# Two blocks of the up projection begun by token halves instead of three, one more by quarters; the context row by transfers, other planner prices, one more block of memory

## The chip, the cores and the metric

The kernel runs on one core of a Trainium2 chip. Its time is the device time of one execution in microseconds; the median of several executions is compared. The core has five engines, each with its own stream of instructions: TensorE (PE) multiplies matrices into eight banks of accumulator memory, VectorE (DVE) and ScalarE (ACT) work element by element, GpSimd (POOL) does the same more slowly, and SyncE (SP) mostly issues transfers between the large memory and the on-chip memory.

## The reference

One layer of a hybrid backbone over 512 latent tokens of width 1024, with 256 context tokens as a prefix. Cut to what matters:

```python
mod_x = split((silu(c)     @ w_mod + b_mod), 6)      # shift, scale, gate for latent tokens
mod_c = split((silu(c_ctx) @ w_mod + b_mod), 6)      # the same for context tokens
h_x = modulate(rms_norm(x,   mix_pre_norm), mod_x[0], mod_x[1]) @ w_in
h_c = modulate(rms_norm(ctx, mix_pre_norm), mod_c[0], mod_c[1]) @ w_in
mix = concat([latent_attention(...), ssd(...)]) @ w_out      # attention and a two-way state-space scan
x = x + mod_x[2] * rms_norm(mix, mix_post_norm)

h = modulate(rms_norm(x, ffn_pre_norm), mod_x[3], mod_x[4])
gate, val = split(h @ w_up, 2)                               # w_up: 1024 x (2 x 2816)
gate = depthwise_conv(gate, conv_w, conv_b)                  # width 3, along the tokens
ffn = (gelu(gate) * val) @ w_down                            # w_down: 2816 x 1024
x = x + mod_x[5] * rms_norm(ffn, ffn_post_norm)
```

All is float32. The kernel keeps that precision on TensorE by splitting each operand into a high and a low part (an ACT copy and a VectorE subtraction, `split`, lines 596 and 597) and adding three products: high x high, high x low, low x high.

## The kernel before

**An order worked out by a planner.** The program is traced twice. In the first pass every piece of memory is its own tile and the instructions are only listed. `plan` then finds the dependences between them, gives each instruction a cost (`price`) and places the pieces in `UNITS` units of 1 KB per partition (four make one block of 4 KB). A piece may reuse units only if the units' old users are modelled to end at least `MARGIN` ns before; units from `EDGE` on are kept for small pieces. A list scheduler, `Graph.schedule`, simulates the five engines and one DMA queue and writes the order of every engine; `plan` does this for 24 rounds, keeps the round with the shortest modelled time, and `refined` tries 1200 random shifts of priority on it. The second pass emits the instructions with each engine's order fixed. So an edit of one place can move instructions everywhere, and a constant of the model changes nothing but the order and the places in memory.

**The order of the stages.** The modulation of the first two chunks is computed while its weights arrive (to about 40 us), then the input projection, the scan and the attention pairs beside each other (to about 500), the output projection (L1436, 502 to 587), the up projection (588 to 830) and the down projection (L1764, to 930). The first 15 us hold matmuls on zeros (L786) that bring up TensorE's clock.

**The rows of `silu(c)`.** `cv` holds `c` in eight rows of 128 and `c_ctx` in eight more; lines 758 and 759 turn it into silu times two. `spread(i, v)` (line 766) copies one of the two over all 128 partitions: eight matmuls with a selecting column as the weight (L770) into a pair of banks, and one ACT copy of 1024 elements (L772). `spread(0, cs)` serves the latent tokens at the start, `spread(1, csc)` the context sums (`moddot`, L695) later.

**The up projection.** The hidden width 2816 is cut into 22 blocks of 128; each block has a gate half and a value half, so two 1024 x 128 weights. `up(j, ...)` with `gemm_T` (L861) computes a block plainly. The first `EARLY` = 3 blocks are begun on token rows 0 and 1 (256 tokens), while rows 2 and 3 are still being normalised (L1518, L1522) and transposed (`transposes`, L1530); their late halves follow. The transposes of rows 2 and 3 stand in the code ahead of the last early block. Each pair of banks comes from a list: what is freed goes to its end and what is needed is taken from its front.

The next 19 blocks follow the string `SEVEN`: 16 times "A", three times "P". "P" is the plain block of 512 tokens. "A" is `up_by_seven`: the product of the 2 x 2 quarters of weight and activation is made with seven quarter products instead of eight (Winograd's form of Strassen's scheme), each of 4 x 3 matmuls of 256 columns (`product`, L1646). It needs mixed activations, made once by `turn_h2` (sums L1597 to L1600, then wide splits), and mixed weights per block, made by `seven`: four loads, one of them an accumulating transfer issued from GpSimd (L1615) that adds two quarters on the way, then two sums on VectorE (L1625, L1626) and four splits. Partial products leave the banks by ACT (L1651) and VectorE (L1662, L1664, L1666). `gated` then does the convolution (L1566, L1567, L1569), gelu (L1571) and the product with the value half (L1573, L1574, or L1576 in a plain block), and for each pair of blocks the mixed operands of the down projection, which goes by seven products too (`sweep`, L1764).

**Small tiles.** `smalls` is a strip of 512 columns from which scalars are cut; `ones` is a 128 x 128 square of ones, read as a weight at L1047 and L1048 and as one column elsewhere.

Of the kernel before, what the change touches and what calls it, by code (L numbers as in the profile page):

```python
# [12 lines left out]
F32 = mybir.dt.float32  # L13
# [6 lines left out]
P = 128  # L20
D = 1024
# [52 lines left out]
    return c  # L74


UNITS, EDGE, MARGIN = 212, 168, 2500
STEP = {1: 1, 2: 2, 3: 4, 4: 4}

ON_PE = 2, 4, 6  # L80
# [1 line left out]
IDLE = 22, 26, 22  # L82
WIDE = 64
PACE = 1.9
TRIES = 1200
HOLD = 6
SEVEN = "AAAAAAAAAAAAAAAAPPP"


class Memory:  # L90
# [66 lines left out]
def price(x):  # L157

    ops = [(v.bass_ap.tensor.name, list(v.ap), v) for l in (x.outs, x.ins) for v in l if hasattr(v, "bass_ap")]
    size = lambda o: math.prod(c for _, c in o[1][1:])  # L160
    e, n = engine_of(x), max(map(size, ops))
    chip = all(not o[0].startswith("banks") for o in ops)
    kind = type(x).__name__
    if "DMA" in kind:
        n = size(ops[0]) * ops[0][1][0][1]
        runs = n // min(o[1][-1][1] for o in ops)
        return max(n * 4 / 360, runs * RUN / 16) * (2 if getattr(x, "cce_op", None) == ALU.add else 1)
    if e == "PE":
        if ops[1][2].dtype == mybir.dt.float32r:
            return (size(ops[1]) / (2.4 if size(ops[1]) >= 256 else 1.2) + 13) / (2 if ops[0][1][0][1] == 64 else 1)  # L170
        return max(107, size(ops[1]) / 1.2) if x.is_transpose else max(213, size(ops[1]) / 0.6)
    if "Memset" in kind:
        return 35 + 0.83 * n
    if e == "Activation":
        return 72 + (43 if chip else 0) + 93 * (len(ops) - 2) + 0.833 * n
    if e == "Pool":
        return 150 + (1.66 if any(not s for o in ops for s, c in o[1][1:] if c > 1) else 2.1) * n
    if "Predicated" in kind:
        return 69 + 1.02 * n
    if "Reciprocal" in kind:  # L180
        return 69 + 6.25 * n
    if "TensorScalar" in kind and chip and sum(size(o) > 1 for o in ops[1:]) < 2:
        return 69 + 0.52 * n
    return (130 if len(ops) == 4 or "TensorScalar" in kind and n > 1 and len(ops) == 3 else 69) + 1.04 * n
# [127 lines left out]
class Graph:  # L312
# [39 lines left out]
    def schedule(self, rank, look=0.06, back=False):  # L352

        eng, dma, cost, tables, shared = self.eng, self.dma, self.cost, self.tables, self.shared
        n, opens, after = len(cost), () if back else self.opens, self.before if back else self.after
        left = [len(b) for b in (self.after if back else self.before)]
        ready, start, end = [0.0] * n, [0.0] * n, [0.0] * n
        PE, SP, POOL, never = ENGINES.index("PE"), ENGINES.index("SP"), ENGINES.index("Pool"), float("inf")
        clock, order = [0.0 if back else BEGIN] * len(ENGINES), [[] for _ in ENGINES]
        later, now, due = [[] for _ in ENGINES], [[] for _ in ENGINES], [never] * len(ENGINES)  # L360
        ticks, held, port, queue, flying = {}, [0 if e == "Activation" else (4, 4) for e in ENGINES], 0.0, 0.0, []
        push, pop = heapq.heappush, heapq.heappop

        def turn(e):
            l, w, t = later[e], now[e], clock[e]
            while l and l[0][0] <= t:
                _, r, i = pop(l)
                push(w, (r, i))
            due[e] = t if w else l[0][0] if l else never

        for i in range(n):
            if not left[i]:
                ready[i] = max(0.0, rank[i] - AHEAD) if i in opens else 0.0
                push(later[eng[i]], (ready[i], rank[i], i))
        for e in range(len(ENGINES)):
            turn(e)
        for _ in range(n):
            while True:
                t = min(due)
                e = due.index(t)  # L380
                l, w = later[e], now[e]
                while l and l[0][0] <= t:
                    _, r, i = pop(l)
                    push(w, (r, i))
                r, i = pop(w)
                near, far, sooner = t + look * cost[i], t + 0.8 * cost[i], None
                for v in l:
                    if v[1] < r and v[0] < (near if v[1] > r - 5000 else far) and (sooner is None or v[1] < sooner[1]):
                        sooner = v
                if sooner is None:  # L390
                    break
                push(w, (r, i))
                clock[e] = sooner[0]
                turn(e)
            order[e].append(i)
            c, d = cost[i], dma[i]
            if not back and tables[i] not in (None, held[e]):
                held[e], t = tables[i], t + (TURN if e == PE else TABLE)
            if shared[i]:
                t = max(t, port)  # L400
                port = t + c
            if d and not back and len(flying) >= FLYING:
                t = max(t, flying[-FLYING])
            start[i] = t
            if d:
                began = t + d + DMA_START + (0 if e == SP else 2500 if e == POOL else 600)
                queue = max(began, queue) + c
                f = queue + DMA_ALONE * c
                if e != SP:
                    clock[e] = t + (1000 if e == POOL else 60)  # L410
                else:
                    if not back and t < DMA_FILLS:
                        f = max(began + (1 + DMA_ALONE) * c, queue - DMA_FULL)
                    clock[e] = t + d if back else max(t + d, queue - DMA_AHEAD)
                flying.append(f + DMA_WAIT)
            elif e == PE:
                f = t + c if back else self.product(t, i, ticks)
                clock[e] = f + 3
            else:
                clock[e] = f = t + c  # L420
            end[i] = f
            turn(e)
            for j, w in after[i]:
                if f + w > ready[j]:
                    ready[j] = f + w
                left[j] -= 1
                if not left[j]:
                    if j in opens:
                        ready[j] = max(ready[j], rank[j] - AHEAD)
                    push(later[eng[j]], (ready[j], rank[j], j))  # L430
                    turn(eng[j])
        return max(end), {e: o for e, o in zip(ENGINES, order)}, start, end
# [40 lines left out]
        return now  # L473


def plan(ins, pieces, hints, units, rounds=24):

# [16 lines left out]
                    preds[i].update(last)  # L496
    opens, shared = {u[0] for u in users.values()}, [ports(x) for x in ins]
    _, _, start, end, _ = Graph(preds, eng, dma, cost, share, tables, urgent, opens, shared).best()
    found = None
    for _ in range(rounds):  # L500
        held, types = [(-1, -1e9, [])] * units, [None] * (units // 4)
        inst, before = [((), -1e9)] * (units // 4), [((), -1e9)] * (units // 4)
        full, places = [set(p) for p in preds], []
        for t, (n, type_), at in pieces:
# [8 lines left out]
                        able.append(o)  # L513
                        free[o], due[o] = max(max(v[1] for v in h), (before if types[b] == type_ else inst)[b][1]), h

            fit = [o for o in able if free[o] + MARGIN <= s0]
            fit = [o for o in fit if (o >= EDGE) == (n < 3)] or fit
            if fit:
                o = max(fit, key=lambda o: sum(v[1] for v in due[o]) / len(due[o]))
# [17 lines left out]
        graph = Graph(full, eng, dma, cost, share, tables, urgent, opens, shared)  # L537
        now = graph.best()
        start, end = ([(p + q) / 2 for p, q in zip(*v)] for v in zip((start, end), now[2:4]))
        if found is None or now[0] < found[0][0]:  # L540
            found = now, places, graph
    now, places, graph = found
    now = graph.refined(now, TRIES)
    return now[0], places, now[1]


# [18 lines left out]
def build(nc, tc, ctx, a, out, dbg=None, places=None):  # L565
# [10 lines left out]
    def c_(shape, name, dt=F32):  # L576
        return cp.tile(list(shape), dt, name=name, tag=name, bufs=1)
# [9 lines left out]
    def load(dst, src, q=None):  # L587
        (q or nc.sync).dma_start(out=dst, in_=src)
# [16 lines left out]
        split(*w, raw, lo_eng)  # L605
        return w

    smalls = c_([P, 512], "smalls")

    def small(tag, w=1):  # L610
        cnt[0] += w
# [65 lines left out]

    sel = c_([P, 32], "sel", F32R)
    V.tensor_copy(sel, C("sel"))
    ones = c_([P, P], "ones")  # L680
    G.memset(ones, 1.0)


# [74 lines left out]
    act(th, cv, AF.Tanh, scale=0.5)  # L758
    V.scalar_tensor_tensor(out=cv, in0=th, scalar=1.0, in1=cv, op0=ALU.add, op1=ALU.mult)
    split(cvp[:16], cvp[32:48], cv)  # L760
    act(cch, cc, AF.Tanh, scale=0.5)
    V.scalar_tensor_tensor(out=cc, in0=cch, scalar=1.0, in1=cc, op0=ALU.add, op1=ALU.mult)
    V.tensor_scalar(out=cc, in0=cc, scalar1=0.5, scalar2=None, op0=ALU.mult)
# [63 lines left out]
    for i in range(NX):  # L827
        silu_of_z(0, zp, i)
    pfree(*za, pmod)
    spread(1, csc)  # L830
    zb = [pget("b"), pget("b"), pget("s"), pget("m")]
    mark = here()
    wz = [weight(a["wz"][k][:, 512:], 512) for k in range(KD)]
# [210 lines left out]
    pc, pt_ = pget("s"), pget("s")  # L1044
    mm(pc[:, :192], lhsT=C("trif"), rhs=fl(aF), start=True, stop=False)
    mm(pc[:, :192], lhsT=C("trib"), rhs=fl(aB), start=False, stop=True)
    mm(pt_[:, :192], lhsT=ones, rhs=fl(aF), start=True, stop=False)  # L1047
    mm(pt_[:, :192], lhsT=ones, rhs=fl(aB), start=False, stop=True)  # L1048
    V.tensor_copy(fl(cum), pc[:, :192])
    V.tensor_tensor(out=nb, in0=lnd, in1=cum, op=ALU.subtract)  # L1050
    V.tensor_tensor(out=fl(sw), in0=pt_[:, :192], in1=fl(nb), op=ALU.add)
# [500 lines left out]

    gT, mixed = [], []
    early, late = slice(0, 256), slice(256, 512)
    EARLY = 3

    h2v = lambda k, p_: h2[p_][k // 2][:, k % 2, :]

# [386 lines left out]
```

## Time and profile before

| what | us |
|---|---|
| median of three runs | 939.51 |
| lowest and highest of them | 938.52, 942.12 |
| the profiled execution | 939.16 |
| its span, first to last instruction | 937.4 |
| up projection, first matmul of L861 | 588.64 |
| output projection's last transposes and first early block: TensorE busy, 550 to 600 | 48.22 of 50 |
| down projection: TensorE busy, 850 to 900 | 49.21 of 50 |

The span is what the trace shows; the execution's own time is 1.76 us longer. The view by stages gives for each stretch the busy time of each engine; a "busy" TensorE means that at least one matmul was in flight, so spacing inside a run of equal matmuls, not the duration of one, is the price of a further one. A group's idle time is what the engine spent waiting just ahead of those instructions, with the releaser that ended it.

### The profile page before, as it was taken

Reading aid. Unit: us, or ns where it says so; the run is one execution under the profiler, and the core shown is the slowest. Engines: PE = TensorE matmul, PEld = TensorE weight load, DVE = VectorE, ACT = ScalarE, POOL = GpSimd, SP = SyncE. Lnnn points to the kernel's source line nnn. Section 1 sums busy time; section 2 is a strip of 40 time slices with the busy share of each in tenths; the row PEclk is TensorE's granted clock in tenths of the full one; section 3 lists DMA queues with packets and bytes.
Section 4 is the critical chain, followed back from the end, with each engine's and each line's share of the span. In section 5 each row is a group of like instructions: output and inputs, shape, how many; then the busy total and the mean of one; then the engine's idle time right before and its main releaser. Section 6 shows DMA issues by size and latency. Waiting matters only on the chain. (4 is left out here: it accounts for less than half of the span.)

```text
span 937.4 us, 16164 instructions
## 1 busy us (share of the span) xinstructions
PE 918.0 (98%) x5678; PEld 815.4 (87%) x5678; DVE 828.6 (88%) x1546; ACT 575.1 (61%) x1138; POOL 224.0 (24%) x230
## 2 busy tenths in 40 slices
PE   9999999999999999999999999999999999999997
PEld 8888898888888888879888888899999999888785
DVE  6999968888989888999999986997889889889998
ACT  4455336645688867868898224964455546357684
POOL 0001000565445665465520010100100000210011
PEclk9999999999999999999999999999999999999999
DMA  9943201114144333244669585924975755885883
GB/s 347 360 161 111 87 23 46 51 51 106 50 96 105 74 96 88 57 127 108 169 209 346 195 279 194 264 70 107 280 202 164 195 124 193 220 205 163 264 294 133
DMA packets 61552, 150.33 MB, mean 160 GB/s; under 512 B 8688, under 2 KB 11904, under 8 KB 61472
## 3 DMA queue, kind: packets, MB, share of 16 engines
q1 hardware_dynamic: 56784, 136.36, 45.7%
q0 software_dynamic: 3888, 11.27, 6.8%
q10 hardware_dynamic: 800, 1.68, 0.6%
q8 instruction: 44, 0.72, 0.3%
q14 instruction: 36, 0.29, 0.1%
HBM read 127.02 MB, written 6.34 MB: 142 GB/s over the span
## 5 line engine op out<-in xcount | busy, mean ns | idle before, releaser
L596 ACT ACTIVATE block<-block 128x512 fp32r<-128x512 f32 (+5 forms) x381 | 245.4, 681 | 144.9 <-DVE block L597 25.1
L597 DVE TENSOR_TENSOR block<-block,block 128x512 fp32r<-128x512 f32 (+4 forms) x357 | 276.7, 807 | 13.8 <-ACT block L596 9.1
L861 PE MATMUL banks<-block,block 128*128 128x512 f32 (+1 forms) x1364 | 277.8, 345 | 3.0 <-DVE smalls L635 1.8
L861 PEld LDWEIGHTS banks<-block,block 128*128 128x128 f32 x1364 | 214.4, 189 | 32.2 <-ACT block L596 3.7
L1646 PE MATMUL banks<-block,block 128*128 128x256 f32 x1344 | 168.3, 284 | 2.2 <-ACT block L596 1.0
L1646 PEld LDWEIGHTS banks<-block,block 128*128 128x128 f32 x1344 | 164.7, 192 | 4.1 <-ACT block L596 1.2
L1764 PE MATMUL banks<-block,block 128*128 128x512 f32 x462 | 109.5, 390 | 0.8 <-ACT block L596 0.6
L1764 PEld LDWEIGHTS banks<-block,block 128*128 128x128 f32 x462 | 86.4, 188 | 19.9 <-ACT block L596 1.2
L1308 PE MATMUL banks<-block,block 128*128 128x512 f32 (+1 forms) x384 | 102.4, 357 | 0.9 <-ACT block L1312 0.7
L596 ACT ACTIVATE block<-banks 128x512 fp32r<-128x512 f32 (+1 forms) x157 | 74.3, 494 | 30.6 <-PE banks L1324 18.9
L597 DVE TENSOR_TENSOR block<-banks,block 128x512 fp32r<-128x512 f32 (+1 forms) x157 | 85.0, 553 | 7.8 <-ACT block L596 7.1
L1436 PE MATMUL banks<-block,block 128*128 128x512 f32 x384 | 89.8, 391 | 0.0
L1436 PEld LDWEIGHTS banks<-block,block 128*128 128x128 f32 x384 | 71.5, 188 | 14.6 <-DVE block L1369 0.2
L1336 PE MATMUL banks<-block,block 128*128 128x256 f32 x384 | 70.1, 292 | 0.7 <-DVE block L1369 0.4
L1324 PE MATMUL banks<-cst,block 128*128 128x128 f32 x384 | 67.4, 274 | 1.1 <-DVE block L597 1.0
L1308 PEld LDWEIGHTS banks<-block,block 128*128 128x128 f32 x384 | 61.8, 189 | 6.8 <-ACT block L1312 1.5
L1310 DVE TENSOR_REDUCE smalls<-banks 128x1 f32<-128x768 f32 x64 | 60.8, 950 | 7.7 <-PE banks L1308 6.9
L695 DVE SCALAR_TENSOR_TENSOR block<-block,block 128x1024 f32<-128x1024 f32 x52 | 63.5, 1234 | 1.8 <-DMA block<-in_wmod_dram 1.8
L1312 ACT ACTIVATE block<-banks,smalls 128x768 f32<-128x768 f32 x64 | 57.8, 903 | 10.4 <-DVE smalls L1310 9.6
L890 DVE SCALAR_TENSOR_TENSOR block<-banks,cwh,block 128x511 f32<-128x511 f32 (+3 forms) x88 | 52.8, 623 | 11.7 <-ACT block L886 10.7
L1336 PEld LDWEIGHTS banks<-block,block 128*128 128x128 f32 x384 | 57.2, 189 | 4.8 <-DVE block L1369 0.8
L1615 POOL DMA_DIRECT2D block<-in_wup_dram x16 | 14.0, 873 | 196.0 <-DMA block<-in_wup_dram 97.4
(258 smaller groups left out, 1225.2 us busy)
## 6 DMA issues: line engine op xcount, KB each, us to landing
block<-in_wmod_dram SPq DMA_DIRECT2D x48, 512.0 KB
block<-in_wup_dram SPq DMA_DIRECT2D x44, 512.0 KB
block<-in_wdn_dram SPq DMA_DIRECT2D x88, 256.0 KB
block<-block SPq DMA_DIRECT2D x32, 256.0 KB
block<-in_wout_dram SPq DMA_DIRECT2D x16, 512.0 KB
block<-in_wup_dram POOLq DMA_DIRECT2D x16, 512.0 KB, 8.0
block<-in_wxbc_dram SPq DMA_DIRECT2D x12, 512.0 KB
block<-block SPq DMA_DIRECT2D x40, 128.0 KB
```

What stands on the lines that cost most here:

```text
L596: act(hi, src, AF.Copy)
L597: (lo_eng or V).tensor_tensor(out=lo, in0=src, in1=hi, op=ALU.subtract)
L695: V.scalar_tensor_tensor(out=junk, in0=wt, scalar=0.5, in1=vec, op0=ALU.mult, op1=ALU.mult, accum_out=acc)
L861: mm(po, lhsT=wf(k, pt[0]), rhs=xf(k, pt[1]), start=(k == 0 and pt == parts[0]), stop=(k == nk - 1 and pt == parts[-1]))
L1308: mm(sc[:, o : o + n], lhsT=q_[:, x_, qi * P : (qi + 1) * P], rhs=kk[:, y_, :], start=part == 0, stop=part == 2)
L1310: V.reduce_max(nm, sc[:, :T], axis=AX.X, negate=True)
L1312: act(pe, sc[:, :T], AF.Exp, bias=nm, scale=1.0, accum_out=sum_)
L1324: nc.tensor.transpose((tx if c < NX else tc_)[:, o : o + P], pe[:, s_ : s_ + P], ident)
L1336: mm(po[:, half * 256 : half * 256 + 256], lhsT=vst(c), rhs=rhs, start=(part == 0 and c == 0), stop=(part == 1 and c == NKT - 1))
L1436: mm(po[i][:, nh * 512 : nh * 512 + 512], lhsT=l[lp][:, i * P : (i + 1) * P], rhs=w[wp][:, nh * 512 : nh * 512 + 512], start=(k == 0 and l ...
L1646: mm(po, lhsT=l[lp][:, k * P : (k + 1) * P], rhs=r(k, rp), start=first and k == n == 0, stop=k == 3 and n == 2, skip_group_check=not first)
L1764: mm(po[i], lhsT=l[:, lp, i * P : (i + 1) * P], rhs=w[wp], start=first and q == 0 and n == 0, stop=q == PAIRS[-1] and n == 2, skip_group_c ...
```

## The change

`EARLY` goes from 3 to 2 and `SEVEN` gets one more "A", so two blocks begin by halves, 17 go by quarters and three stay plain. The context row `csc` is no longer spread by TensorE but written to a row in the large memory and read back to all partitions, both on SP's queue. `ones` shrinks to one column that is read as a broadcast weight, and `smalls` to 164 columns; `UNITS` goes from 212 to 216, one block more, which lies among the units for small pieces.

The rest is the planner: the margin of a round is drawn from three values; 36 rounds instead of 24; the best five rounds get 200 tries, the best two of them 400 more, the best one 600 more. An accumulating transfer is priced at three times its bytes instead of two, and one issued from GpSimd is modelled to begin earlier (1000 ns after its issue) and to land 3000 ns later.

```diff
-UNITS, EDGE, MARGIN = 212, 168, 2500
+UNITS, EDGE, MARGIN = 216, 168, (1500, 2500, 4000)
...
-TRIES = 1200
+TRIES = (5, 200), (2, 400), (1, 600)
...
-SEVEN = "AAAAAAAAAAAAAAAAPPP"
+SEVEN = "AAAAAAAAAAAAAAAAAPPP"
...
-        return max(n * 4 / 360, runs * RUN / 16) * (2 if getattr(x, "cce_op", None) == ALU.add else 1)
+        return max(n * 4 / 360, runs * RUN / 16) * (3 if getattr(x, "cce_op", None) == ALU.add else 1)
...
-                began = t + d + DMA_START + (0 if e == SP else 2500 if e == POOL else 600)
+                began = t + d + (DMA_START + (0 if e == SP else 600) if e != POOL else 1000)
                 queue = max(began, queue) + c
-                f = queue + DMA_ALONE * c
+                f = queue + DMA_ALONE * c + (3000 if e == POOL else 0)
...
-def plan(ins, pieces, hints, units, rounds=24):
+def plan(ins, pieces, hints, units, rounds=36):
...
-    found = None
+    found, chance = [], random.Random(1)
     for _ in range(rounds):
+        margin = chance.choice(MARGIN)
...
-            fit = [o for o in able if free[o] + MARGIN <= s0]
+            fit = [o for o in able if free[o] + margin <= s0]
...
-        if found is None or now[0] < found[0][0]:
-            found = now, places, graph
-    now, places, graph = found
-    now = graph.refined(now, TRIES)
+        found.append((now, places, graph))
+    for tries in TRIES:
+        found = sorted(found, key=lambda f: f[0][0])[: tries[0]]
+        found = [(g.refined(now, tries[1]), p, g) for now, p, g in found]
+    now, places, graph = min(found, key=lambda f: f[0][0])
...
-    smalls = c_([P, 512], "smalls")
+    smalls = c_([P, 164], "smalls")
...
-    ones = c_([P, P], "ones")
+    ones = c_([P, 1], "ones")
...
+    row = nc.dram_tensor("context_row", (1, KD, P), F32, kind="Internal").ap()
...
-    spread(1, csc)
+    load(row[0], cv[KD:])
+    load(csc, row.rearrange("o k p -> o (k p)").to_broadcast([P, D]))
...
-    mm(pt_[:, :192], lhsT=ones, rhs=fl(aF), start=True, stop=False)
-    mm(pt_[:, :192], lhsT=ones, rhs=fl(aB), start=False, stop=True)
+    mm(pt_[:, :192], lhsT=ones.to_broadcast([P, P]), rhs=fl(aF), start=True, stop=False)
+    mm(pt_[:, :192], lhsT=ones.to_broadcast([P, P]), rhs=fl(aB), start=False, stop=True)
...
-    EARLY = 3
+    EARLY = 2
```

## The prediction

> **What bounds the kernel now.** I read the page first, then the time by stages, then what TensorE waits for, then its timeline.
>
> ```profile
> span 937.4 us, 16164 instructions
> PE 918.0 (98%) x5678; PEld 815.4 (87%) x5678; DVE 828.6 (88%) x1546; ACT 575.1 (61%) x1138; POOL 224.0 (24%) x230
> ...
> 0.00:50.00 50.00, 47.74 (x291) 43.47 (x292) 41.40 (x99) 24.99 (x44) 0.84 (x8) 1.00 0.97 357
> 600.00:650.00 50.00, 50.00 (x418) 49.95 (x417) 45.43 (x66) 32.79 (x53) 2.59 (x3) 1.00 0.42 109
> 900.00:938.00 38.00, 30.44 (x135) 24.81 (x133) 33.62 (x73) 22.95 (x56) 9.07 (x6) 0.96 0.54 185
> ...
> 882.04 48.40 PE L1764 MATMUL banks<-block,block 128*128 128x512 f32 x212 [0.23 <-DVE block L597]
> ```
>
> In the stage rows the columns after the stage's length are busy times of TensorE (PE), weight loads, VectorE (DVE), ScalarE (ACT) and GpSimd, the granted clock, the DMA share and GB/s. TensorE is busy 918.0 of 937.4 us, so 19.4 us are idle. Its last matmul ends at 882.04 + 48.40 = 930.44, so 7.0 us of those are the tail in which the last rows are normalised and stored; 12.4 lie in the middle. The middle is a string of small stalls: the view of TensorE's waits has 18 kinds, of which the first and the last stand here, and below them three from the timeline, with the idle time ahead of each run in brackets:
>
> ```profile
> PE banks L861 <- DVE smalls L635: 1.8, 1, 1.8
> ...
> PE banks L1336 <- DVE block L597: 0.2, 1, 0.2
> ...
> 690.27 13.11 PE L1646 MATMUL banks<-block,block 128*128 128x256 f32 x106 [0.36 <-DVE block L1573]
> 704.16 35.48 PE L1646 MATMUL banks<-block,block 128*128 128x256 f32 x292 [0.79 <-DVE block L597]
> 740.67 46.59 PE L1646 MATMUL banks<-block,block 128*128 128x256 f32 x384 [1.03 <-ACT block L596]
> ```
>
> So TensorE's work sets the time: each us of matmul taken away is a us gained, as long as nothing behind it becomes late. What could become late is seen in finer stages around the start of the up projection:
>
> ```profile
> 588.00:600.00 12.00, 11.36 (x95) 11.24 (x96) 11.79 (x34) 11.92 (x44) 1.29 (x1) 1.00 1.03 277
> 600.00:610.00 10.00, 10.00 (x86) 10.00 (x85) 10.00 (x18) 10.00 (x20) 0.88 (x1) 1.00 0.81 225
> 620.00:630.00 10.00, 10.00 (x85) 10.00 (x85) 9.96 (x12) 5.43 (x6) 0.00 (x0) 1.00 0.01 2
> 640.00:650.00 10.00, 10.00 (x85) 10.00 (x85) 6.22 (x13) 3.57 (x7) 0.00 (x0) 1.00 0.09 37
> ```
>
> VectorE is as full as TensorE from 588 to 630 and has room again only after 640. This is the place where the change works.
>
> **The block that goes from halves to quarters, on TensorE.** A block begun by halves is two weights x 8 parts of the contraction x 3 products x 2 token halves = 96 matmuls of 256 columns (L861). A block by quarters is 7 products x 4 parts x 3 = 84, also of 256 columns (L1646). The price of each is the spacing inside a long run:
>
> ```profile
> 599.09 6.60 PE L861 MATMUL banks<-block,block 128*128 128x256 f32 x53
> ...
> 639.83 50.07 PE L1646 MATMUL banks<-block,block 128*128 128x256 f32 x415
> ```
>
> A run's length less the last one's 0.28 us, over the count less one: (6.60 - 0.28) / 52 = 0.1215 and (50.07 - 0.28) / 414 = 0.1203 us. The early block costs 96 x 0.1215 = 11.7 us, the quartered one 84 x 0.1203 = 10.1. **Term: -1.6 us**. Its edges are -1.4 (both kinds at 0.1203) and -1.7.
>
> **The context row.** `spread(1, csc)` goes: eight 128-column matmuls and one ACT copy (L772). Two transfers come instead.
>
> ```profile
> 54.77 0.56 PE L770 MATMUL banks<-block,sel 128*128 128x128 f32 x4
> 55.17 0.67 PE L793 MATMUL banks<-block,block 128*128 128x512 f32 x2
> ...
> 3.96 0.28 DVE L759 SCALAR_TENSOR_TENSOR block<-block 16x128 f32<-16x128 f32 x1 [3.96 <-ACT block L758]
> ...
> 58.49 1.22 DVE L695 SCALAR_TENSOR_TENSOR block<-block,block 128x1024 f32<-128x1024 f32 x1
> ...
> 41.64 1.44 SPq L588 DMA_DIRECT2D block<-in_wcq_dram  x2
> 52.81 0.33 SPq L588 DMA_DIRECT2D block<-in_wkd_dram  x1
> ...
> 557.36 3.78 DMA mod_rows<-block
> ...
> 548.86 8.18 DMA block<-mod_rows
> ```
>
> Four take 0.40 us up to the next instruction, eight twice that: **-0.8 us**. The new pair has not run here; its nearest relatives are the rows of the modulation, which were written in up to 3.78 us and read to all partitions in up to 8.18, so about 12 us one behind the other. Its source is ready at 4.2, and its first reader is a context sum on VectorE at 58.49, so 54 us stand against 12. On SP's queue the read waits for the write, and whatever SP issues next waits behind it, up to 3.8 us: here SP issues nothing from 43.1 to 52.81, and the loads behind (kd and third cq weight) are for matmuls after 57. The 512 KB that the read moves cost 1.5 us at the 357 GB/s of the first stage if they fall before 50, nothing after. I take 0 for it, bounds 0 to +1.5, because the free SP stretch is the nearest row.
>
> **The work that covers the second token half.** With two early blocks instead of three, TensorE has less to do while token rows 2 and 3 are still being normalised, transposed and split.
>
> ```profile
> 588.64 0.50 PE L861 MATMUL banks<-block,block 128*128 128x256 f32 x2 [1.78 <-DVE smalls L635]
> ...
> 590.83 0.60 PE L1530 MATMUL banks<-cst,block 128*128 128x128 f32 x4
> ...
> 589.73 0.63 ACT L1503 ACTIVATE block<-banks 128x512 f32<-128x512 f32 x1
> ...
> 603.38 0.75 DVE L597 TENSOR_TENSOR block<-block,block 128x256 fp32r<-128x256 f32 x2
> ```
>
> The cover starts at 588.64: 96 early-half matmuls x 0.1215 = 11.7, and the transposes of rows 1 to 3, at most 24 at 0.11 (the four at 590.83: 0.60 less the last one's 0.27, over 3) = 2.6, so it lasts to 602.9. The last split of the late tokens ends at 603.38 + 0.75 = 604.1. The gap of 1.2 us is filled by late-half products over the first parts of the contraction, whose splits end earlier. Cost 0, at most +1.2. The bank pairs rotate differently too: the transposes of row 2 now take row 3's pair, which ScalarE has read by 589.73 + 0.63 = 590.4, ahead of the 590.83 at which they ran; they wait for nothing new.
>
> **VectorE there.** By the groups of the stage 588 to 840:
>
> ```profile
> L597 DVE TENSOR_TENSOR block<-block,block 128x1024 fp32r<-128x1024 f32 x59 | 70.9, 1217 | 4.6 <-PE banks L1646 2.8 <-ACT block L596 1.6
> L1625 DVE TENSOR_TENSOR block<-block,block 128x512 f32<-128x512 f32 x16 | 10.9, 683 | 4.6 <-PE banks L1646 4.6
> L1567 DVE SCALAR_TENSOR_TENSOR block<-block,prm,block 128x511 f32<-128x511 f32 x15 | 11.2, 745 | 3.3 <-ACT block L1566 3.3
> L1662 DVE TENSOR_TENSOR block<-banks,block 128x256 f32<-128x256 f32 x16 | 6.5, 414 | 0.2 <-PE banks L1646 0.2
> ...
> 588.00:640.00 52.00, 16.59 (x117) 15.22 (x118) 1.00 0.62 162
> ...
> 588.00:640.00 52.00, 2.74 (x4) 1.00 0.62 162
> ```
>
> The quartered block has three 1024-wide splits (1.20 each), one of 512 and two sums of 512 (0.68 each), and five steps of 256 (0.41) where the early one has two wide splits and one step of 0.68: 7.7 against 3.1, **4.6 us more on VectorE** while TensorE has 1.6 less. The last two rows are L1646 and L1625 alone: by 640 TensorE had run 117 / 84 = 1.4 quartered blocks and VectorE had prepared four (one L1625 each). That lead of 2.6 blocks, about 14 us of its work, is the cover. The change spends 11.7 / 10.1 = 1.2 blocks of it by starting quarters that much earlier, and 4.6 us (0.8 block) more; about half a block is left. I take 0.
>
> **The rest.** The 17th block by quarters fetches 1.75 MB instead of 1 MB, one of its four loads an accumulating one from GpSimd; the DMA share of 0.42 from 600 to 650 covers it. The thinner `ones` and `smalls` and the fourth small-piece block cost nothing by themselves. The planner's prices move no work on the chip; they change the order that it writes. Accumulating loads are now priced to land later, and the three stalls at 690 to 741 (0.36 + 0.79 + 1.03 = 2.2 us) hang, in the chain, on such loads:
>
> ```profile
> 674.17 9.32 DMA block<-in_wup_dram
> ```
>
> The longer search and 4 KB more per partition can take some of the other stalls, or make new ones. I take half of those 2.2, **-1.1**, with bounds of +3 and -5 from the 12.4 us in the middle: another order won't reach none of them, and a new one has as many places to go wrong.
>
> **Sum.** The profiled execution took 939.16 us, 1.8 beside its span and 0.35 under the median of the runs, 939.51. 939.16 - 1.6 - 0.8 - 1.1 = 935.7, and as the median stands 0.35 above that execution, 936.0. A measurement of this kernel tells 0.5% from no change, that is 4.7 us: 934.8 and 944.2 are the borders.
>
> **Rivals.** *The new order heals more of the stalls.* For it: from 620 to 630 DMA stands still (0.01) because no piece of memory is free, and a further block is granted. Against it: 18 separate waits of at most 1.8 us. Half of the 12.4 gone: 939.2 - 2.4 - 6.2 = 930.6; with a third, 932.7.
>
> *VectorE becomes the bound at the start of the quarters* (the slower side). After both early blocks TensorE stands at 602.9 + 11.7 = 614.6; the first products of one quartered block that need no mixed operand (24 x 0.12) carry it to 617.5. Then it needs `turn_h2`: eight steps of 0.68 and four wide splits, 10.3 us of VectorE.
>
> ```profile
> 598.57 0.68 DVE L1625 TENSOR_TENSOR block<-block,block 128x512 f32<-128x512 f32 x1
> ...
> 615.26 3.48 DVE L597 TENSOR_TENSOR block<-block,block 128x1024 fp32r<-128x1024 f32 x3
> ```
>
> Here the wide splits that can belong to it ended by 615.26 + 3.48 = 618.7 at the latest, about level with 617.5. If the new order puts the weights of two or three blocks (5.6 each) and two gates (two convolution steps of 0.75 and one of 0.68, 2.2 each) ahead, then from 598.6, where L1625 first ran in the stage, the mixed operands come at 598.6 + 10.3 + 11.3 + 4.3 = 624.5, or 630 with three: a wait of 7 to 13 us. At 10 it gives 939.2 - 2.4 + 10 = 946.8; it makes the kernel slower by the border from about 7.4, mixed operands at 625. Against it: the old order had the same choice and put `turn_h2` first.
>
> *Accumulating loads are held up where VectorE is full.* They took 5.2, 8.0 and 12.4 us to land (least, median, most):
>
> ```profile
> DMA to landing us min/median/max: 5.2/8.0/12.4
> ...
> 602.21 0.88 POOL L1615 DMA_DIRECT2D block<-in_wup_dram  x1 [10.48 <-DMA block<-in_wup_dram]
> ```
>
> If the earlier quarters meet a landing of 12.4 instead of 8.0, TensorE waits 4.4: 936.0 + 4.4 = 940.4. Against it, GpSimd's issue at 602.21, with VectorE at 10.00 of 10, took the usual 0.9. The Trainium skill, page "SBUF — State Buffer", section "SBUF: two separate sides", speaks for it: a load issued from GpSimd can stand still while VectorE's two-port operations keep GpSimd from writing its descriptors. By that rule the extra accumulating load sits in the worst stretch; this trace's 0.88 us issue doesn't show it.
>
> *The gain is swallowed.* After 834 the chain runs through VectorE's splits of the down projection; if that work, not TensorE's arrival, paces the end, the 2.4 us turn into idle time: 939.2.
>
> **How the numbers follow.** Forecast 0.36, new order heals more 0.34, gain swallowed 0.12, accumulating loads 0.10, VectorE the bound 0.08. The forecast's own spread, and the accumulating and swallowed cases, stay inside the borders; of the healing case a sixth does too, of the forecast a tenth falls under 934.8, and of the VectorE case a fifth stays in. So faster 0.32, same 0.61, slower 0.07. The range takes the healing case down to 931.5 and the unfavourable bounds (+1.5, +1.2, half of +3) up to 940.5; some 0.1 lies under it and 0.1 above.
>
> **What would show it.** Right: L770 has 8 matmuls, L1646 1428, L861 with 256 columns 96 fewer than 640; TensorE busy 2 to 2.5 us less, and its idle middle between 8 and 14. VectorE still full at 588 to 640, with no wait of L1646 on L1597 to L1600 or on their splits. Wrong: such a wait above 3 us, a wait of VectorE on `context_row` near 58, or stalls from 690 on as long as before.

## The result and the profile after

The changed kernel takes 932.18 us, median of 5 executions (930.34 to 933.60), against 938.52 for the kernel before, median of 5. The ratio is 0.9923, with a 95% interval of 0.9903 to 0.9942: 5.4 to 9.1 us faster. The forecast was 936.0 against 939.51, a ratio of 0.9963. The direction was right and the size about half: 3.5 us were forecast, and 0.9923 of 938.52 is 7.2 us less. The same kernel run again later (e5 below) gave 0.9937, 5.9 us less.

The page of the changed kernel, and below it the last stretch of TensorE's timeline (start, length, engine and line, operands, count, and in brackets the idle time ahead). The kernel's lines are numbered two to four higher: `split` is L598 and L599, `gemm_T` L865, the quarter products L1650, the down projection L1768.

```profile
span 930.4 us, 16165 instructions
PE 915.9 (98%) x5658; PEld 812.0 (87%) x5658; DVE 825.8 (89%) x1554; ACT 578.1 (62%) x1142; POOL 220.2 (24%) x231
```

```profile
874.68 48.93 PE L1768 MATMUL banks<-block,block 128*128 128x512 f32 x212 [0.23 <-DVE block L599]
```

TensorE is busy 915.9 us instead of 918.0. Its last matmul ends at 923.61, so the tail is 6.8 us against 7.0 before, and 930.4 - 915.9 - 6.8 = 7.7 us of idle time are left in the middle, where there were 12.4. Of the 7.0 us that the span lost, 2.1 are busy time, 4.7 idle time in the middle and 0.2 tail. The view by stages shows where; first the kernel before, then the changed one, the first busy time being TensorE's:

```profile
150.00:200.00 50.00, 49.33 (x283) 42.47 (x282) 41.61 (x69) 28.83 (x49) 23.60 (x20) 1.00 0.15 47
300.00:350.00 50.00, 49.19 (x321) 43.14 (x320) 44.09 (x71) 37.18 (x83) 29.73 (x30) 1.00 0.38 89
400.00:450.00 50.00, 48.48 (x318) 42.27 (x318) 46.57 (x93) 39.04 (x92) 31.92 (x31) 1.00 0.45 114
550.00:600.00 50.00, 48.22 (x263) 41.49 (x262) 35.74 (x77) 29.08 (x74) 4.02 (x4) 1.00 0.78 246
700.00:750.00 50.00, 48.18 (x396) 47.57 (x395) 44.26 (x73) 28.64 (x44) 3.90 (x6) 1.00 0.63 176
```

```profile
150.00:200.00 50.00, 50.00 (x292) 43.40 (x291) 41.83 (x70) 29.42 (x52) 23.42 (x21) 1.00 0.21 63
300.00:350.00 50.00, 49.91 (x329) 43.34 (x327) 43.95 (x70) 37.74 (x83) 31.53 (x32) 1.00 0.34 90
400.00:450.00 50.00, 49.54 (x333) 44.03 (x332) 47.06 (x101) 40.47 (x95) 27.24 (x30) 1.00 0.42 106
550.00:600.00 50.00, 49.53 (x279) 42.98 (x278) 38.39 (x78) 29.43 (x78) 5.05 (x5) 1.00 0.85 265
700.00:750.00 50.00, 50.00 (x418) 49.95 (x417) 41.52 (x65) 25.59 (x40) 3.44 (x4) 1.00 0.57 147
```

The first three stages are attention and scan, more than 130 us ahead of the up projection. Of their lines only the four short matmuls with the broadcast `ones` were edited (near 166 us), and they give 0.7 + 0.7 + 1.1 = 2.5 us of the 4.7. So it was the new order, with its places in memory, that did that; e5, another execution of the same code, has 50.00, 49.93 and 49.58 there. The up projection's start (550 to 600) gives 1.3, but the stage ahead of it loses 0.7 (49.27 of 50 against 50.00). The stage of the last two stalls that the forecast halved (700 to 750) gives 1.8, and 0.4 is lost from 650 to 700, where a stall of 0.75 stands at 657.

```profile
585.90 0.50 PE L865 MATMUL banks<-block,block 128*128 128x256 f32 x2 [0.47 <-ACT block L598]
...
657.60 118.64 PE L1650 MATMUL banks<-block,block 128*128 128x256 f32 x983 [0.75 <-ACT block L1655]
```

These are TensorE's timeline: the first early matmul waits 0.47 instead of 1.78, and from 657.60 on 983 quarter matmuls run without a stop.

### The profile page after: what moved, and what is told of

Same layout as the page of the kernel before. It is cut to its first block, busy times and chain, and to the rows that moved or that the text cites. A ratio compares the mean times of both kernels' runs of the same rounds, so it can differ in the third digit from the quotient of the medians.

```text
span 930.4 us, 16165 instructions
## 1 busy us (share of the span) xinstructions
PE 915.9 (98%) x5658; PEld 812.0 (87%) x5658; DVE 825.8 (89%) x1554; ACT 578.1 (62%) x1142; POOL 220.2 (24%) x231
## 5 line engine op out<-in xcount | busy, mean ns | idle before, releaser
L598 ACT ACTIVATE block<-block 128x512 fp32r<-128x512 f32 (+5 forms) x383 | 247.1, 681 | 131.2 <-PE banks L1650 18.2
L599 DVE TENSOR_TENSOR block<-block,block 128x512 fp32r<-128x512 f32 (+4 forms) x359 | 277.7, 805 | 18.7 <-ACT block L598 9.7
L865 PE MATMUL banks<-block,block 128*128 128x512 f32 (+1 forms) x1268 | 263.6, 349 | 0.5 <-ACT block L598 0.5
L865 PEld LDWEIGHTS banks<-block,block 128*128 128x128 f32 x1268 | 203.6, 189 | 28.6 <-ACT block L598 1.0
L1650 PE MATMUL banks<-block,block 128*128 128x256 f32 x1428 | 178.7, 283 | 0.8 <-ACT block L1655 0.8
L1650 PEld LDWEIGHTS banks<-block,block 128*128 128x128 f32 x1428 | 175.2, 192 | 2.0 <-ACT block L1655 1.0
L1768 PE MATMUL banks<-block,block 128*128 128x512 f32 x462 | 108.0, 391 | 0.6 <-ACT block L598 0.3
L1768 PEld LDWEIGHTS banks<-block,block 128*128 128x128 f32 x462 | 86.1, 188 | 20.3 <-DVE block L599 1.7
L1312 PE MATMUL banks<-block,block 128*128 128x512 f32 (+1 forms) x384 | 98.0, 355 | 0.2 <-ACT block L1316 0.2
L599 DVE TENSOR_TENSOR block<-banks,block 128x512 fp32r<-128x512 f32 (+1 forms) x157 | 85.5, 554 | 11.1 <-ACT block L598 9.2
L598 ACT ACTIVATE block<-banks 128x512 fp32r<-128x512 f32 (+1 forms) x157 | 75.0, 492 | 21.8 <-PE banks L1328 8.9
L1340 PE MATMUL banks<-block,block 128*128 128x256 f32 x384 | 69.6, 295 | 0.0
L894 DVE SCALAR_TENSOR_TENSOR block<-banks,cwh,block 128x510 f32<-128x510 f32 (+3 forms) x88 | 51.6, 622 | 13.5 <-ACT block L890 12.9
```

The costliest lines, as they stand in the source:

```text
L598: act(hi, src, AF.Copy)
L599: (lo_eng or V).tensor_tensor(out=lo, in0=src, in1=hi, op=ALU.subtract)
L865: mm(po, lhsT=wf(k, pt[0]), rhs=xf(k, pt[1]), start=(k == 0 and pt == parts[0]), stop=(k == nk - 1 and pt == parts[-1]))
L1312: mm(sc[:, o : o + n], lhsT=q_[:, x_, qi * P : (qi + 1) * P], rhs=kk[:, y_, :], start=part == 0, stop=part == 2)
L1340: mm(po[:, half * 256 : half * 256 + 256], lhsT=vst(c), rhs=rhs, start=(part == 0 and c == 0), stop=(part == 1 and c == NKT - 1))
L1650: mm(po, lhsT=l[lp][:, k * P : (k + 1) * P], rhs=r(k, rp), start=first and k == n == 0, stop=k == 3 and n == 2, skip_group_check=not first)
```

## The experiments

The question is which part gives the gain: the work (fewer matmuls on TensorE), the prices, the search or the memory. All ratios are to the kernel before on the same chip, with their 95% intervals; 0.001 is 0.94 us. An idle middle is that of one profiled execution of each kernel, and it moves: the changed kernel has 7.7 us in the profile above and 11.5 in that of e5, which took 937.60 us where e5's median is 932.93. The profiles of e2 and e17 too are of the longest of their twelve executions.

### One part undone at a time

e1 takes the old search back:

```diff
-UNITS, EDGE, MARGIN = 216, 168, (1500, 2500, 4000)
+UNITS, EDGE, MARGIN = 216, 168, 2500
-TRIES = (5, 200), (2, 400), (1, 600)
+TRIES = 1200
-def plan(ins, pieces, hints, units, rounds=36):
+def plan(ins, pieces, hints, units, rounds=24):
...
```

> The changed kernel with the old search alone: 24 rounds, one margin of 2500, 1200 tries on the best round. Before 938.5, after 932.2; TensorE's idle middle was 12.4 us and is 7.7. Theory SEARCH (the longer search found an order with fewer stalls, all through the kernel): TensorE's work stays near 915.9 and the idle middle returns to about 12, so 936 to 937. Theory MEMORY (the added block of 4 KB let transfers start earlier): 932 to 933, idle 8. Theory PRICES (accumulating transfers priced later): 932 to 933, idle 8.

Measured: 937.63, ratio 1.0001 (0.9987 to 1.0014); idle middle 11.0, TensorE busy 918.6. The whole gain is gone, though the removed matmuls are still removed. With another seed (e18 below) half of it stays.

e2 takes the old prices back:

```diff
-        return max(n * 4 / 360, runs * RUN / 16) * (3 if getattr(x, "cce_op", None) == ALU.add else 1)
+        return max(n * 4 / 360, runs * RUN / 16) * (2 if getattr(x, "cce_op", None) == ALU.add else 1)
...
-                began = t + d + (DMA_START + (0 if e == SP else 600) if e != POOL else 1000)
+                began = t + d + DMA_START + (0 if e == SP else 2500 if e == POOL else 600)
...
-                f = queue + DMA_ALONE * c + (3000 if e == POOL else 0)
+                f = queue + DMA_ALONE * c
```

> The changed kernel with the old prices of accumulating and GpSimd-issued transfers. Theory PRICES: the three stalls ahead of quarter products at 690 to 741 come back, 2.2 us, so 934 to 935. Theories SEARCH and MEMORY: 932 to 933, with at most 1 us of such stalls.

Measured: 936.59, ratio 0.9982 (0.9966 to 0.9998); idle middle 12.1, 1.5 of it between 650 and 700. More was lost than the three stalls, whose return was expected to give 934 to 935.

e3 takes the memory back:

```diff
-UNITS, EDGE, MARGIN = 216, 168, (1500, 2500, 4000)
+UNITS, EDGE, MARGIN = 212, 168, (1500, 2500, 4000)
```

> The changed kernel with 212 units instead of 216. Theory MEMORY: idle middle 10 to 12 us, so 935 to 937. Theories SEARCH and PRICES: 932 to 933, idle 7 to 9.

Measured: 932.86, ratio 0.9953 (0.9935 to 0.9971); idle middle 8.3. The memory isn't what the gain hangs on.

e4 takes the block back:

```diff
-SEVEN = "AAAAAAAAAAAAAAAAAPPP"
+SEVEN = "AAAAAAAAAAAAAAAAPPP"
...
-    EARLY = 2
+    EARLY = 3
```

> The changed kernel with three blocks begun by halves and 16 by quarters. By the prediction's term TensorE's busy time rises by 1.6 us (96 matmuls at 0.1215 against 84 at 0.1203), so 933.8 if the idle middle stays at 7.7. If the better order came from the changed start of the up projection, the idle middle also rises, to 10 or more, and the time to 936 or more.

Measured: 935.85, ratio 0.9970 (0.9952 to 0.9988); idle middle 9.9. It looked as if the early block cost twice its matmuls. e16 below shows that it doesn't.

### How far one order stands from another

e5 is the changed kernel once more; e6 and e7 differ in one seed each, so the work is the same to the last matmul:

```diff
-    found, chance = [], random.Random(1)
+    found, chance = [], random.Random(2)
...
-        chance = random.Random(3)
+        chance = random.Random(4)
```

(The first pair of lines is e6, the second e7.)

> The changed kernel as it is, beside the others of this call, so that they are compared on one chip. All theories: ratio to before about 0.9923, as measured; 931 to 933.

> The changed kernel with another seed (2 for 1) for the margins drawn in the 36 rounds: the same work, prices, memory and length of search, another order. Theory LUCK (each order that the search happens on has its own stalls, some us apart, whatever the constants): the time moves by 2 us or more from the unchanged one, with TensorE's idle middle. Theory SEARCH (a longer search reliably ends near the same time): within 1.5 us of it.

> The changed kernel with another seed (4 for 3) for the random tries: again the same work, another order. LUCK: 2 us or more away from the unchanged one or from the other seed. SEARCH: within 1.5 us of both.

Measured: 0.9937 (0.9913 to 0.9960), 0.9918 (0.9897 to 0.9940) and 0.9927 (0.9900 to 0.9954). Three orders of one search lie within 0.002. That spoke against luck; it was too early to say so, as the next pairs show.

e8 is the planner's side alone on the work of before:

```diff
-UNITS, EDGE, MARGIN = 212, 168, 2500
+UNITS, EDGE, MARGIN = 216, 168, (1500, 2500, 4000)
...
-TRIES = 1200
+TRIES = (5, 200), (2, 400), (1, 600)
...
     EARLY = 3
```

with the 36 rounds, prices, `smalls` and `ones` of the change.

> The kernel before with all of the planner's side of the change (longer search, prices, memory with the thinner tiles) and none of the work's side: three blocks by halves, 16 by quarters, the row spread by TensorE. If the planner's side gave the gain beyond the removed matmuls (SEARCH): TensorE's busy time near 918, idle middle about 8, ratio 0.995, 933.5 to 934.5. If the gain needs the changed work or is the luck of one order (LUCK): 936 to 939.

Measured: 937.51, ratio 0.9974 (0.9955 to 0.9993). e9 is the work's side alone on the planner of before (two early blocks, 17 by quarters, the row by transfers):

```diff
-SEVEN = "AAAAAAAAAAAAAAAAPPP"
+SEVEN = "AAAAAAAAAAAAAAAAAPPP"
...
-    spread(1, csc)
+    load(row[0], cv[KD:])
+    load(csc, row.rearrange("o k p -> o (k p)").to_broadcast([P, D]))
...
-    EARLY = 3
+    EARLY = 2
```

> The kernel before with the work's side alone (two early blocks, 17 by quarters, the context row by transfers), and the planner, prices and memory of before. By the prediction's terms -2.4 us, ratio 0.9974, if removed matmuls are gained under any order. If search and prices must come together to keep the gain (what old search 1.000 and old prices 0.998 point to), nothing is left of it: ratio 0.999 to 1.003 and an idle middle of 13 us or more.

Measured: 937.46, ratio 0.9999 (0.9979 to 1.0019). e10 is the search alone at the old prices (the lines of e1, the other way, on the kernel before, with its 212 units):

> The kernel before with the longer search alone, at the old prices. Theory SEARCH alone: the idle middle falls to about 8, ratio 0.995. Theory SEARCH WITH PRICES (a longer search at prices that are wrong finds orders that are short only in the model): ratio 0.998 to 1.003.

Measured: 936.83, ratio 0.9983 (0.9963 to 1.0003); idle middle 11.7. e11 spreads the row by TensorE again in the changed kernel:

```diff
-    load(row[0], cv[KD:])
-    load(csc, row.rearrange("o k p -> o (k p)").to_broadcast([P, D]))
+    spread(1, csc)
```

> The changed kernel with the context row spread by TensorE again. By the prediction's term +0.8 us on the changed kernel's 932.2 to 932.9: 933 to 934, ratio 0.9945. If another order moves it as undoing the early block did (3 us for a term of 1.6): 935.

Measured: 933.79, ratio 0.9952 (0.9936 to 0.9969): the expected size, but no larger than what seeds do. e12 searches longer still:

```diff
-TRIES = (5, 200), (2, 400), (1, 600)
+TRIES = (8, 300), (3, 800), (1, 2000)
-def plan(ins, pieces, hints, units, rounds=36):
+def plan(ins, pieces, hints, units, rounds=60):
```

> The changed kernel with a longer search still: 60 rounds, the best eight get 300 tries, the best three 800, the best one 2000. SEARCH: a further 1 to 2 us below the changed kernel, 930 to 931.5, ratio 0.991, idle middle 6 to 7. If the model is exhausted (its errors are as large as what a search can still find): 932, as the two other seeds.

Measured: 932.93, ratio 0.9940 (0.9922 to 0.9959). The expected 0.991 didn't come: nothing more is found on the chip.

By then the parts seemed to need each other: work alone nothing, planner alone 2.4 us, both 6 to 7. Six more kernels repeat five of the variants, and the kernel before, with another seed (that of the rounds, as in e6, for e13, e16 and e17; that of the tries, as in e7, for e14, e15 and e18), to tell that from the luck of one order.

> The planner's side alone (as e8, ratio 0.9974) with the other seed for the rounds. INTERACTION (the planner's side is worth 2.4 us without the changed work): 0.997 to 0.998. LUCK (e8 drew a poor order): 0.995 or less, 934 or less.

> The work's side alone (as e9, ratio 0.9999) with the other seed for the tries. INTERACTION (the old planner loses the removed work again): 0.999 to 1.001. LUCK: 0.997, the predicted 2.4 us, or elsewhere.

> The kernel before with the other seed for the tries, nothing else. It measures the luck of one order of the old search: within 0.0015 of 1 if orders of one search lie close, as the changed kernel's three did (0.9918 to 0.9937); 2 us or more away if not.

> The changed kernel with three early blocks and 16 by quarters (as e4, ratio 0.9970) and the other seed for the rounds. If the early block costs its matmuls and no more: 0.9947 (0.9930 of the changed kernel's three orders, + 1.6 us). If its cost is what e4 showed: 0.997.

> The changed kernel with the old prices (as e2, ratio 0.9982) and the other seed for the rounds. PRICES (a search at the old prices finds orders that are short only in the model): 0.997 to 0.999. LUCK of e2's order: 0.994 or less.

> The changed kernel with the old search (as e1, ratio 1.0001) and the other seed for its tries. SEARCH: 0.999 to 1.001. LUCK of e1's order: 0.996 or less.

| variant | first order | other seed |
|---|---|---|
| before | 1 | e15: 0.9987 (0.9970 to 1.0005) |
| work alone | e9: 0.9999 | e14: 1.0019 (0.9999 to 1.0039) |
| changed, old search | e1: 1.0001 | e18: 0.9961 (0.9944 to 0.9978) |
| changed, old prices | e2: 0.9982 | e17: 0.9976 (0.9956 to 0.9995) |
| planner's side alone | e8: 0.9974 | e13: 0.9939 (0.9921 to 0.9956) |
| changed, three early blocks | e4: 0.9970 | e16: 0.9913 (0.9899 to 0.9926) |

So one seed moves a variant by up to 0.0057, 5 us (e4 against e16): more than the 2.4 us of matmuls. What stands out from that is the split by prices and search, each kernel counting once and the changed one twice:

| | old search | longer search |
|---|---|---|
| old prices | 1, e15, e9, e14: mean 1.0001 | e2, e17, e10: mean 0.9980 |
| new prices | e1, e18: mean 0.9981 | changed, e5 to e8, e3, e4, e11, e12, e13, e16: mean 0.9941 |

The four with neither have the old memory as well. The eleven with both lie between 0.9913 and 0.9974, the nine others between 0.9961 and 1.0019. With both the gain is there without the changed work too: e13 has all the matmuls of before and 0.9939, e16 has three early blocks and is the lowest of all at 931.34, though its interval overlaps the changed kernel's, so it isn't shown to beat it. The work's own 2.4 us can't be told from these scatters: the six full variants with both (changed, e3, e5, e6, e7, e12) have a mean of 0.9933, the four without the 17th quartered block (e4, e8, e13, e16) 0.9949, 1.5 us; and on the old planner the work gave nothing (mean of e9 and e14 1.0009, of before and e15 0.9994). Whether the memory is worth the 2 us that e3 suggests stays open, with one order only.

TensorE's idle middle splits more sharply by the prices than the times do. It is 6.7 to 11.5 us in the thirteen profiles with new prices, 8.6 in the mean, and 10.4 to 14.4 in the seven with old ones, 12.3 in the mean. The search moves it little: means of 12.1 and 12.7 at the old prices, 9.6 and 8.5 at the new. Nor is it the memory: e2 and e17 have the new memory at old prices (12.1 and 14.4), e3 the old memory at new prices (8.3). The prices are two edits, the factor on the bytes and the times of a GpSimd issue; no run separates them, nor the parts of the search.

### What the prices mend

e17 shows one stall that hangs on loads, in the longest of its twelve executions (940.61 us, median 936.51), in the timelines of GpSimd, SP, ScalarE and TensorE (start, length, engine and line, operands, count, and in brackets the idle time ahead with its releaser).

```profile
697.45 0.86 POOL L1619 DMA_DIRECT2D block<-in_wup_dram  x1 [5.17 <-PE banks L1650]
700.54 0.86 POOL L1619 DMA_DIRECT2D block<-in_wup_dram  x1 [2.23 <-PE banks L1650]
...
699.35 10.43 SPq L590 DMA_DIRECT2D block<-in_wup_dram  x4
...
709.78 1.57 ACT L598 ACTIVATE block<-block 128x1024 fp32r<-128x1024 f32 x2 [5.22 <-DMA block<-in_wup_dram]
...
711.68 12.39 PE L1650 MATMUL banks<-block,block 128*128 128x256 f32 x80 [2.56 <-ACT block L1655]
```

In its chain of waits, between the last quarter matmul before the stall and the first after it, stand these:

```profile
699.35 10.40 DMA block<-in_wup_dram
...
710.74 0.61 ACT block L598
711.35 0.28 ACT block L1655
...
711.68 9.04 PE banks L1650 x52
```

Two accumulating loads are issued around 699.35, where SP begins four plain ones. All share the DMA engines, which stand at 0.99 of their time from 700 to 710, and the plain load of 699.35 takes 10.40 us to land. ScalarE's split of that weight is at the head of ScalarE's queue and waits 5.22; behind it stands L1655, which takes a quarter product out of its bank; and TensorE waits 2.56 for that bank. So an accumulating load can matter through the loads beside it. That it was the price that put this load and its reader too close is argued, not shown. Work alone with the old prices (e14, profiled near its median) has the same at 692.90, with 11.25 us to land and 3.69 us of TensorE's time. Between 600 and 800 the seven kernels with old prices idle 0.1 to 3.7 us, 1.8 in the mean; the thirteen profiles with new prices 0 to 1.8, 0.5 in the mean. That is part of the prices' effect; the rest is spread.

Nor does three times the bytes measure better than two. The page of the changed kernel splits the time of the DMA engines by queue (packets, MB, share of the 16 engines), and the second row holds the 28 accumulating loads and nothing else:

```profile
q1 hardware_dynamic: 57216, 137.15, 46.5%
q0 software_dynamic: 4032, 11.80, 7.6%
```

Per MB that is 0.34% for the first and 0.64% for the second, so 1.9 times. The new prices do better without being nearer to this; perhaps they act as a reserve.

## Why the prediction was right in sign and short in size

**The bound.** TensorE's end sets the time, as read. "Each us of matmul taken away is a us gained" was only argued, and the runs don't bear it out: e9 and e14 took the matmuls away and gained nothing. Under a planner that reorders the whole program, the us went into other stalls.

**The terms of the work.** The counts came as worked out: 1428 quarter matmuls, 544 of 256 columns in `gemm_T` (96 fewer), 8 instead of 16 in `spread`; busy time fell by 2.1 where 2.4 was forecast. That agreement is in part luck: in e5 the same matmuls are busy 917.5 us, only 0.5 less than before. That the time fell by the same 2.1 is not shown by any pair of kernels.

**The context row.** SP's queue waited for the row's write, 4.8 us, somewhat more than the 3.8 that was put as the most; the read was issued at 48.44 and the first context sum ran at 56.81 without a wait. Cost 0, as taken. The row of SP's waits (us in total, times, longest), and VectorE's timeline:

```profile
SPq L590 <- DMA context_row<-block: 4.8, 1, 4.8
```

```profile
56.81 1.21 DVE L697 SCALAR_TENSOR_TENSOR block<-block,block 128x1024 f32<-128x1024 f32 x1
```

**The cover and VectorE.** The step's result was right and its size wrong. VectorE was full as forecast. Stages of the changed kernel, of all work and then of two lines alone:

```profile
607.00:617.00 10.00, 10.00 (x86) 10.00 (x85) 10.00 (x14) 9.41 (x13) 0.00 (x0) 1.00 0.33 101
637.00:647.00 10.00, 10.00 (x86) 10.00 (x85) 10.00 (x18) 5.08 (x9) 0.86 (x1) 1.00 0.91 264
```

```profile
585.00:637.00 52.00, 29.89 (x217) 27.94 (x218) 1.00 0.69 189
...
585.00:637.00 52.00, 3.43 (x5) 1.00 0.69 189
```

The last two rows are the quarter matmuls and the first weight sum (L1629) alone: 217 / 84 = 2.6 blocks run and five prepared in 52 us. A lead of 2.4 blocks is left, not half a block, and VectorE is full from 637 to 647, where the kernel before had room. The slower rival, mixed operands that come late, didn't happen.

**Accumulating loads held up by VectorE.** They landed in 5.3, 7.0 and 9.5 us (least, median, most) against 5.2, 8.0 and 12.4. The rule of the Trainium skill, page "SBUF — State Buffer", section "SBUF: two separate sides", that VectorE's two-port operations can keep GpSimd from writing a load's descriptors, was weighed as a rival. The load that was late in e17 is a plain one issued by SP, which the rule isn't about; the DMA engines stood at 0.99 there, which speaks for contention among loads. Whether VectorE ever held up an accumulating load isn't shown.

**The new order: the step that failed.** "The planner's prices move no work on the chip" is true, and from it I priced the order at 1.1 us, half of three stalls that were said to hang on accumulating loads. That reading holds for the first of the three alone. In the chain of the kernel before, the second ends on VectorE's split, and the third's load follows an issue by SP, so it is a plain one:

```profile
702.97 1.15 DVE block L597
...
724.88 0.38 SPq L588
725.26 0.05 issue
725.31 8.23 DMA block<-in_wup_dram
```

The idle middle fell by 4.7 us between the two profiles where 1.1 was forecast, and by 3.7 in the mean of all kernels with new prices against old. The step left out that the order is written for the whole program, so that more than half of the 4.7 lay in attention and scan. By the table, search and prices alone are each worth 2 us and both 5.6; whether together they give more than their sum isn't shown, with two or three kernels in a corner. The rival "the new order heals more of the stalls", with half or a third of the 12.4 us gone and 930.6 to 932.7, is what happened in this pair (4.7 is 38%, and leaves 7.7, just under the 8 to 14 that were given as a sign of being right). It had nearly the same chance, 0.34 against 0.36, held down because the stalls were many and small; small ones went all through the program.

**Busy is not work.** The bounds for the new order were taken from the 12.4 us of idle time in the middle, as if busy time couldn't move. The profiles of kernels with the very same matmuls (changed, e1 to e3, e5 to e7, e9, e12, e14, e17, e18) show TensorE busy between 913.9 and 919.9. A part of a stall can hide inside it, as the last section shows.

## What to carry to other kernels

Where a planner orders the program, its cost model and search are a part of the kernel like any other: ask first how much idle time the bottleneck engine has in all, and give a change of the model a share of all of it. Before an edit is credited with a few us, run it and its opposite under a second seed; here the seed alone was worth up to 5 us, twice the edit. What a kind of transfer takes of the DMA engines can be read from the page's queue rows before its price is set; here a price above it did better, and why isn't shown.

## What the runs showed of the hardware

A stall of TensorE can cost more than its length. In e17 the stage after the 2.56 us wait, and for comparison the stage before both stalls:

```profile
690.00:700.00 10.00, 10.00 (x86) 10.00 (x85) 6.50 (x11) 5.36 (x9) 0.98 (x2) 1.00 0.77 207
...
710.00:720.00 10.00, 8.32 (x48) 8.33 (x49) 5.60 (x12) 5.24 (x8) 0.97 (x2) 0.66 0.60 155
```

The granted clock falls to 0.66, and the run of 80 matmuls from 711.68 takes 12.39 us where 80 x 0.1203 = 9.6 were due: 2.8 us more, counted as busy. The Trainium skill, page "TensorE: Matmul & The Clock Gate", section "Part 1: The HAM clock gate (the "warmup" mystery)", has TensorE fall to half its clock after an idle window of about 3.4 us; here the waits were 0.78 and 2.56, 3.3 us in two pieces. In steps of 1 us the granted clock is 0.50 from 711 to 717, so the half clock agrees, and 1.00 again from 718. That an idle time of 3.4 us is needed isn't shown: a shorter one stands ahead of the fall in what follows, and the 1.78 us ahead of 588.64 in the kernel before left the clock at 1.00.

A fall of the clock is seen near the start too, in some executions of one and the same program. First the changed kernel's timeline of TensorE and its stage from 10 to 15, then both of e5, the same code:

```profile
12.25 2.88 PE L789 MATMUL banks<-block 128*128 128x256 f32 x22
```

```profile
10.00:15.00 5.00, 3.87 (x33) 3.67 (x32) 3.80 (x22) 1.90 (x4) 0.00 (x0) 1.00 1.03 412
```

```profile
13.07 4.38 PE L789 MATMUL banks<-block 128*128 128x256 f32 x22
```

```profile
10.00:15.00 5.00, 3.34 (x23) 3.17 (x22) 3.80 (x19) 2.18 (x5) 0.00 (x0) 0.85 0.95 340
```

Ahead of the run of zeros that should keep the clock up, TensorE had waited 1.13 us in the one and 1.66 in the other. The 22 matmuls take 2.88 or 4.38, and the first product of weights starts 2.2 us later (19.43 or 21.66). That is 2.2 of the 5.4 us between these two executions (932.18 and 937.60); another 2.2 are idle time from 450 to 550 (TensorE busy 98.13 or 95.93 of 100). So executions of one program differ by some us, and differences of that size need several executions of each kernel.
